# Sums of transformed weights written in place, three accumulating loads under way, and other prices in the order

## The chip, the cores and the metric

The kernel runs on one core of a Trainium2 chip. The metric is the time on the device of one execution, in microseconds (us); the profiled execution's span, from its first instruction to its last, is given beside its time. The engines are TensorE (PE; PEld is its weight loading), VectorE (DVE), ScalarE (ACT), GpSimd (POOL) and SyncE (SP), each with an in-order queue of its own.

## The reference

One step of an encoder of two layers over a prompt of 512 tokens and a sample of 64, which share all weights (width 1024). A layer is an FFN, a mixer with three kinds of attention, attention over a memory of 256 tokens, and a second FFN; outputs are both activations and all new cache entries.

```python
def half_ffn(x, g, w_gate, w_up, w_down):
    h = rms_norm(x, g)
    return 0.5 * ((jax.nn.silu(h @ w_gate) * (h @ w_up)) @ w_down)

x = x + half_ffn(x, p['ffn1_norm'], p['ffn1_w_gate'], p['ffn1_w_up'], p['ffn1_w_down'])
...
x = x + merge_heads(oa, ob, oc, p['b_sub_norm'], p['w_out'], lam_init)
...
x = x + memory_attention(x, mk, mv, p)
x = x + half_ffn(x, p['ffn2_norm'], p['ffn2_w_gate'], p['ffn2_w_up'], p['ffn2_w_down'])
```

Everything is float32. D_FF is 2816, so the four FFNs hold most of the products.

## The kernel before

Activations lie transposed, features on the 128 partitions and the 576 tokens as columns, in two halves of 288. Each float32 factor is split into a high part (float32r, `whi` of a weight, written by a copy) and the rest (`wlo`, a subtraction), and a product is three matmuls: high by high, high by low, low by high. Splitting a weight tile of 512 columns is one copy on ScalarE or VectorE and one subtraction on VectorE; there are eight buffers each for the high and the low parts.

Most FFN products (`gate`, `up` from tile 4 on, and all `down`) multiply 2 x 2 blocks with seven products in place of eight (`wino`): a unit covers a pair of output tiles, and k pairs of input tiles (4 for gate and up, 2 or 3 for down), with n = 128 k columns to a quadrant of its weights. A raw load brings three quadrants (a12, a11, a22) into `stage`, 1536 columns at most, of which there are 2 buffers. A second load brings 2n columns into `wcd` (tag "wc", 2 buffers), and a third, issued by GpSimd, adds the rest of the weights to it under way; that gives c3 and c1. Two sums then make c2 = c1 + a11 and c4 = c2 + a12, into tiles named `wc` that come from the large buffers "b" (11 of 896 columns). The adds may run on VectorE or GpSimd. In the order of the record a unit is: splits of a11 and a12 and their products, the sums, c2, c3, c1, c4, a22. The products go into the banks P, Q and Y; after the first and later products of P its contents are evacuated (`cw`, `dw`, `c` by ScalarE, or a VectorE operation on `x`) before the next product adds to the same bank. In the FFN, eight of the "b" buffers hold the transformed activations `xbh` and `xbl`; in the mixer "b" holds keys and values.

The program is recorded as a list of operations (`Program.op`) and then put in order by a list planner (`Program.order`) that has a price for each operation, a time for each dependence, and the number of buffers of each tag. A step takes the operation that can start first; where an operation may run on two engines, it takes the one that would end first, with 300 ns added for VectorE. Operations of VectorE with two inputs in SBUF, and all that read SBUF on GpSimd, are planned one after another (`port`). A load's data is planned for `late` after its transfer. A `reach` says how far ahead of the oldest open operation a tag's buffers may be taken, by how many are free; names in `free_reach` are exempt, and `quota` bounds how many buffers a name may hold. Weight loads are planned some 9 us ahead of their product, those of `wino` units 3 us more. The order that comes out is issued as it is, and semaphores keep the dependences, so the planner's prices decide the order of each queue and nothing else. All instructions carry line 414, that of `issue`, so the rows are told apart by tiles.

Of the kernel before, what the change touches and what calls it, by code (L numbers as in the profile page):

```python
# [10 lines left out]
F32 = mybir.dt.float32  # L11
F32R = mybir.dt.float32r
AF = mybir.ActivationFunctionType
ALU = mybir.AluOpType
# [4 lines left out]
SP = 512  # L19
# [157 lines left out]
class View:  # L177
# [29 lines left out]
    def split(self, n):  # L207
        (m, st), = self.dims
        return View(self.tile, self.part, self.off, [(n, st * (m // n)), (m // n, st)], self.dtype, self.path + (("split", n),))
# [23 lines left out]
class Program:  # L233


    def __init__(self):
        self.ops = []
        self.pos = 0.0
        self.shift = 0.0
        self.tiles = []  # L240
        self.free_reach = ("wc", "xbh", "xbl")
        self.shared = True
        self.extra = {"DVE": 300.0}
        self.quota = {"wc": 6}
        self.reach = {"s": (-12000.0, 3000.0), "b": (-12000.0, 4000.0)}

    def tile(self, tag, shape, dtype, name):
        t = Tile(tag, shape, dtype, name)
# [36 lines left out]
    def order(self, slots, window=60000.0, depth=24):  # L285
# [8 lines left out]
        def push(o):  # L294
            for e in o.costs:
                heapq.heappush(ready[e], (o.prio, o.start, o))
# [34 lines left out]
        while len(out) < len(self.ops):  # L331
            while byprio[oldest].done:
                oldest += 1
            front = byprio[oldest].prio
            limit = front + window
            best = None
            for e in ENGINES:
                h = ready[e]
                seen, pick = [], None
                while h and len(seen) < depth:  # L340
                    item = heapq.heappop(h)
                    o = item[2]
                    if o.done:
                        continue
                    seen.append(item)
                    if item[0] > limit:
                        break
                    t = estimate(o, e)
                    if t is None:
                        continue  # L350
                    if len(o.costs) > 1:
                        mine = t + o.costs[e] + self.extra.get(e, 0.0)
                        if any(e2 != e and estimate(o, e2) + o.costs[e2] + self.extra.get(e2, 0.0) < mine for e2 in o.costs):
                            continue
                    if pick is None or t < pick[0] - 1.0:
                        pick = (t, o)
                        if t <= free[e] + 1.0:
                            break
                for item in seen:
                    heapq.heappush(h, item)  # L360
                if pick is not None and (best is None or pick[0] < best[0]):
                    best = (*pick, e)
            if best is None:
                names = {}
                for t in self.tiles:
                    if id(t) in place and t.left:
                        names.setdefault(t.tag, {}).setdefault(t.name, 0)
                        names[t.tag][t.name] += 1
                raise RuntimeError(f"no instruction can go on; tiles held: {names}")
            t, o, e = best  # L370
            for x in o.tiles:
                if x.tag is not None and id(x) not in place:
                    heapq.heappop(avail[x.tag])
                    held[x.name] = held.get(x.name, 0) + 1
                if id(x) not in place:
                    place[id(x)] = True
            end = t + o.costs[e]
            free[e] = end
            if e in o.port:
                port = end  # L380
            o.ends = (e, end)
            o.done = True
            out.append((o, e))
            if o.dma:
                dma = max(end + 650.0, dma) + o.extra
                late = 900.0 if e == "SP" else 2900.0
                o.extra = dma + late - end
                end = dma + late
            for x in o.tiles:
                x.last = max(x.last, end)  # L390
                x.left -= 1
                if not x.left and x.tag is not None:
                    heapq.heappush(avail[x.tag], x.last)
                    held[x.name] -= 1
            for u in o.users:
                u.wait -= 1
                if not u.wait:
                    push(u)
# [24 lines left out]


def pool_cost(n):
    return 154 + 2.09 * n


def copy_cost(src):
# [1 line left out]


class Trunk:
    N_S = 46
    N_B = 11
    STAGE = 2
    WC = 2
    WB = 8

    def __init__(self, a):  # L440
# [14 lines left out]
        return self.new("s", [128, T], dt, nm)  # L455

    def bl(self, dt=F32R, nm="b"):
        return self.new("b", [128, 896], dt, nm)

    def tiny(self, nm="t"):  # L460
        return self.new("tiny", [128, 4], F32, nm)
# [113 lines left out]
    def ahead(self):  # L575
        return -self.AHEAD * self.p.pos / (self.p.pos + self.AHEAD) - 900.0
# [43 lines left out]
    def wino(self, movs, sinks):  # L620

        p = self.p
        n = 128 * len(movs)

        def ahead(f, *k, early=0.0):
            keep, p.shift = p.shift, self.ahead() - early
            r = f(*k)  # L630
            p.shift = keep
            return r

        def load():
            raw, _, src = self.fetch()
            c31 = self.new("wc", [128, 1024], F32, "wcd")[:, :2 * n]
            self.load(c31, src[:, n:3 * n])
            src, _, _ = self.unit_source()
            self.gather(c31, src)
            return raw, c31  # L640

        def sums(raw, c31):
            if 2 * n <= 896:
                c24 = self.bl(F32, "wc")
                c2, c4 = c24[:, :n], c24[:, n:2 * n]
            else:
                c2, c4 = self.bl(F32, "wc")[:, :n], self.bl(F32, "wc")[:, :n]
            self.tt(c2, c31[:, n:], raw[:, n:2 * n], ALU.add, self.WADD)
            self.tt(c4, c2, raw[:, :n], ALU.add, self.WADD)
            if 2 * n <= 512:  # L650
                return c24[:, :2 * n],
            return c2, c4

        raw, c31 = ahead(load, early=self.EARLY)
        w = {}

        def split(names, src):
            hi, lo = ahead(self.parts, src)
            for i, nm in enumerate(names):
                w[nm] = hi[:, n * i:n * i + n], lo[:, n * i:n * i + n]  # L660

        def product(ps, nm, i, first, last):
            hi, lo = w[nm]
            for k, mov in enumerate(movs):
                xhi, xlo = mov[i]
                o = slice(128 * k, 128 * k + 128)
                self.mms([(ps, lhs[:, o], x, first and k == 0 and j == 0, last and k == len(movs) - 1 and j == 2, False)
                          for j, (lhs, x) in enumerate(((hi, xhi), (hi, xlo), (lo, xhi)))])

        both = 2 * n <= 512  # L670
        if both:
            split(("a12", "a11"), raw[:, :2 * n])
        else:
            split(("a11",), raw[:, n:2 * n])
        P = self.bank("P")[:, :288]
        product(P, "a11", 0, True, False)
        sinks[0](P)
        if not both:
            split(("a12",), raw[:, :n])
        Q = self.bank("Q")[:, :288]  # L680
        product(Q, "a12", 1, True, True)
        sinks[1](Q)
        c = ahead(sums, raw, c31)
        if both:
            split(("c2", "c4"), c[0])
        else:
            split(("c2",), c[0])
        product(P, "c2", 4, False, False)
        sinks[2](P)
        if both:  # L690
            split(("c3", "c1"), c31)
        else:
            split(("c3",), c31[:, :n])
        Y = self.bank("Y")[:, :288]
        product(Y, "c3", 5, True, False)
        if not both:
            split(("c1",), c31[:, n:])
        product(P, "c1", 3, False, False)
        sinks[3](P, Y)
        if not both:  # L700
            split(("c4",), c[1])
        product(P, "c4", 2, False, True)
        sinks[4](P)
        split(("a22",), raw[:, 2 * n:])
        product(Y, "a22", 6, False, True)
        sinks[5](Y)
# [487 lines left out]
    def mix(self, l):  # L1194
# [50 lines left out]
        self.load(self.rope, a["rope"])  # L1245
        self.maskc = self.sl(nm="maskc")[:, :SP]
        self.load(self.maskc, a["maskc"])
        self.kpe = self.new("wc", [128, 1024], F32, "kpe")
        self.memset(self.kpe[96:128], 0.0, "POOL")
        proj(1)  # L1250
        attend_a(1)
# [15 lines left out]
        for g in range(2, GROUPS):  # L1267
            if g < 4:
# [6 lines left out]
                for ps, c in self.gemm("ukv", u[0], cko, KH):  # L1275
                    n = c.stop - c.start
# [7 lines left out]
                for ps, c in self.gemm("ukv", u[1], cko, KH):  # L1284
                    n = c.stop - c.start
# [151 lines left out]
            self.ffn(l, 2, ("ffn1_norm", l + 1) if l + 1 < DEPTH else None)  # L1437

    def slots(self):
        return {"s": self.N_S, "b": self.N_B, "tiny": 24, "sm": 8, "stage": self.STAGE, "hi": self.WB, "lo": self.WB, "wc": self.WC}  # L1440


def build(tc, a):
# [159 lines left out]
```

## Time and profile before

| what | value |
|---|---|
| time, median of 3 runs | 2491.7 us (2484.65 to 2495.42) |
| profiled execution | 2488.79 us, of it the span 2487.0 us |
| TensorE busy | 2405.7 us, 97% |
| VectorE busy | 2113.8 us, 85% |
| ScalarE busy | 1549.1 us, 62% |
| GpSimd busy | 487.6 us, 20% |
| moved by DMA | 316.00 MB, 127 GB/s |

The busy times are of the profiled execution and overlap; the ends of matmuls are modelled. A stretch is read as its length and, for each engine, the time in which it was busy. The FFN units with sums run in four stretches, about 60 to 416 us, 885 to 1244, 1310 to 1648 and 2116 to 2487; mixer, memory attention and the first FFN tiles lie between.

### The profile page before, as it was taken

To read this page: it belongs to the slowest core of one execution; us is meant where nothing else is said; L and a number is where in the kernel's file an instruction comes from. 1 tells how busy PE (TensorE), PEld (TensorE's weight loads), DVE (VectorE), ACT (ScalarE), POOL (GpSimd) and SP (SyncE) were. 2 spreads that over 40 slices of the span, in tenths; PEclk is the share of its full clock that TensorE was granted. 3 is DMA by queue.
4 is the path that set the end of the run, shared out by engine and by line. 5 is a ranking of instruction groups with operands and counts; after the bars stand their busy time and mean duration, and the time that the engine had idled before them with its cause. 6 is when DMAs were issued, how large, how long until landed. Compare 5 with 4: busy or idle time off the path is not lost.

```text
span 2487.0 us, 46756 instructions
## 1 busy us (share of the span) xinstructions
PE 2405.7 (97%) x17622; PEld 2333.4 (94%) x17622; DVE 2113.8 (85%) x4276; ACT 1549.1 (62%) x3266; POOL 487.6 (20%) x500
## 2 busy tenths in 40 slices
PE   8899999999999999999999999999999999999998
PEld 8899999998999999999999999899989999999998
DVE  8888889789896898888898888896898869888887
ACT  5555666679765755556556555576887566555554
POOL 1122220101120122222112332210112101322220
PEclk9899999999999999999999999999999999999999
DMA  4556565222342245566536566641223322365664
GB/s 154 136 153 157 156 166 155 71 70 78 106 141 77 69 114 145 147 165 177 131 105 162 138 162 159 173 136 64 74 86 116 119 69 79 106 170 142 167 169 118
DMA packets 104242, 316.00 MB, mean 127 GB/s; under 512 B 11856, under 2 KB 16016, under 8 KB 104016
## 3 DMA queue, kind: packets, MB, share of 16 engines
q1 hardware_dynamic: 82128, 252.19, 30.5%
q0 software_dynamic: 21888, 60.83, 14.5%
q8 instruction: 138, 2.26, 0.4%
q14 instruction: 88, 0.72, 0.1%
HBM read 300.11 MB, written 12.86 MB: 126 GB/s over the span
## 4 chain that ended last, share of the span: by engine, by line
PE 58%; DVE 25%; DMA 9%; ACT 5%; issue 2%; POOL 0%; SPq 0%; DVEq 0%; ACTq 0%; POOLq 0%
PE P L414 17%; PE Y L414 8%; DVE wlo L414 7%; PE pj L414 7%; DMA wcd<-wf 5%; PE wo L414 4%; PE Q L414 4%; DMA stage<-wf 3%; DVE c L414 3%; PE mq L414 2%; PE mo L414 2%; PE g L414 2%; DVE x L414 2%; DVE wc L414 2%; PE O L414 2%
## 5 line engine op out<-in xcount | busy, mean ns | idle before, releaser
L414 ACT ACTIVATE whi<-stage 128x512 fp32r<-128x512 f32 (+2 forms) x565 | 335.4, 600 | 297.8 <-PE P L414 76.1
L414 DVE TENSOR_TENSOR wlo<-stage,whi 128x512 fp32r<-128x512 f32 (+2 forms) x658 | 434.4, 672 | 94.3 <-ACT whi L414 90.5
L414 POOL DMA_DIRECT2D wcd<-wf x152 | 134.9, 892 | 676.9 <-DVE wlo L414 292.6
L414 ACT ACTIVATE whi<-wc 128x512 fp32r<-128x512 f32 (+1 forms) x236 | 145.0, 614 | 110.2 <-PE P L414 53.5
L414 ACT ACTIVATE whi<-wcd 128x512 fp32r<-128x512 f32 (+1 forms) x232 | 140.6, 612 | 70.7 <-DMA wcd<-wf 23.9
L414 DVE TENSOR_TENSOR wlo<-wc,whi 128x512 fp32r<-128x512 f32 (+1 forms) x240 | 171.5, 714 | 15.2 <-ACT whi L414 14.4
L414 DVE TENSOR_TENSOR wlo<-wcd,whi 128x512 fp32r<-128x512 f32 (+1 forms) x240 | 169.2, 709 | 11.0 <-ACT whi L414 10.8
L414 PE MATMUL pj<-xhi,whi 128*128 128x288 f32 x576 | 172.0, 299 | 2.7 <-DVE pt L414 2.7
L414 PE MATMUL P<-xbh,whi 128*128 128x288 f32 x576 | 170.6, 296 | 2.9 <-ACT cw L414 1.7
L414 PE MATMUL P<-xbl,whi 128*128 128x288 f32 x576 | 170.0, 295 | 0.3 <-DVE xbl L414 0.3
L414 PE MATMUL P<-xbh,wlo 128*128 128x288 f32 x576 | 170.1, 295 | 0.0
L414 PE MATMUL pj<-xhi,wlo 128*128 128x288 f32 x576 | 169.7, 295 | 0.0
L414 PE MATMUL pj<-xlo,whi 128*128 128x288 f32 x576 | 169.7, 295 | 0.0
L414 POOL TENSOR_TENSOR wc<-wcd,stage 128x256 f32<-128x256 f32 (+2 forms) x71 | 88.0, 1240 | 263.9 <-DMA wcd<-wf 146.0
L414 ACT ACTIVATE dw<-P 128x288 f32<-128x288 f32 x240 | 96.2, 401 | 48.2 <-PE P L414 48.2
L414 PEld LDWEIGHTS P<-xbh,whi 128*128 128x128 f32 x576 | 108.1, 188 | 4.5 <-ACT cw L414 2.7
L414 PEld LDWEIGHTS pj<-xhi,whi 128*128 128x128 f32 x576 | 108.1, 188 | 4.5 <-issue 4.2
L414 ACT ACTIVATE cw<-P 128x288 f32<-128x288 f32 x216 | 85.5, 396 | 41.6 <-PE P L414 41.6
L414 PE MATMUL P<-hbh,wlo 128*128 128x288 f32 x352 | 105.6, 300 | 3.5 <-DVE wlo L414 3.5
L414 PEld LDWEIGHTS P<-xbl,whi 128*128 128x128 f32 x576 | 108.1, 188 | 0.6 <-DVE xbl L414 0.6
L414 PEld LDWEIGHTS pj<-xlo,whi 128*128 128x128 f32 x576 | 108.1, 188 | 0.4
L414 PEld LDWEIGHTS P<-xbh,wlo 128*128 128x128 f32 x576 | 108.2, 188 | 0.0
(495 smaller groups left out, 9435.9 us busy)
## 6 DMA issues: line engine op xcount, KB each, us to landing
stage<-wf SPq DMA_DIRECT2D x125, 512.0 KB, 3.5
stage<-wf SPq DMA_DIRECT2D x72, 768.0 KB, 4.2
wcd<-wf SPq DMA_DIRECT2D x72, 512.0 KB, 3.6
wcd<-wf POOLq DMA_DIRECT2D x72, 512.0 KB, 6.3
stage<-wf SPq DMA_DIRECT2D x68, 384.0 KB, 4.0
wcd<-wf SPq DMA_DIRECT2D x64, 256.0 KB, 2.8
wcd<-wf POOLq DMA_DIRECT2D x64, 256.0 KB, 5.7
stage<-wf SPq DMA_DIRECT2D x16, 576.0 KB, 4.2
```

The source lines that it names most:

```text
L414: getattr(eng[e], fn)(**{n: real(v) for n, v in k.items()})
```

## The change

The buffers of tag "wc" are gone. `wcd` is taken from "b", whose 11 buffers grow from 896 to 1024 columns, at most three of them at a time. The two sums write over the raw quadrants that they read, c2 over a11 and c4 over a12, so their tiles `wc` are gone as well; for small units the split of both takes them in that order. `kpe`, the rotary key of the mixer, moves from "wc" to "b". One more "s" buffer (47) is made. In the planner, loads are taken to land 1000 ns later, GpSimd's elementwise price goes from 154 + 2.09 to 250 + 4.5 ns per column, and the reach of "b" begins at -4000 in place of -12000 ns, so that the last free buffers may be taken earlier.

```diff
--- before.py
+++ after.py
@@ -238,11 +238,11 @@
         self.pos = 0.0
         self.shift = 0.0
         self.tiles = []
-        self.free_reach = ("wc", "xbh", "xbl")
+        self.free_reach = ("wcd", "xbh", "xbl")
         self.shared = True
         self.extra = {"DVE": 300.0}
-        self.quota = {"wc": 6}
-        self.reach = {"s": (-12000.0, 3000.0), "b": (-12000.0, 4000.0)}
+        self.quota = {"wcd": 3}
+        self.reach = {"s": (-12000.0, 3000.0), "b": (-4000.0, 4000.0)}
 
     def tile(self, tag, shape, dtype, name):
         t = Tile(tag, shape, dtype, name)
@@ -383,7 +383,7 @@
             out.append((o, e))
             if o.dma:
                 dma = max(end + 650.0, dma) + o.extra
-                late = 900.0 if e == "SP" else 2900.0
+                late = 1900.0 if e == "SP" else 3900.0
                 o.extra = dma + late - end
                 end = dma + late
             for x in o.tiles:
@@ -423,7 +423,7 @@
 
 
 def pool_cost(n):
-    return 154 + 2.09 * n
+    return 250 + 4.5 * n
 
 
 def copy_cost(src):
@@ -431,10 +431,9 @@
 
 
 class Trunk:
-    N_S = 46
+    N_S = 47
     N_B = 11
     STAGE = 2
-    WC = 2
     WB = 8
 
     def __init__(self, a):
@@ -455,7 +454,7 @@
         return self.new("s", [128, T], dt, nm)
 
     def bl(self, dt=F32R, nm="b"):
-        return self.new("b", [128, 896], dt, nm)
+        return self.new("b", [128, 1024], dt, nm)
 
     def tiny(self, nm="t"):
         return self.new("tiny", [128, 4], F32, nm)
@@ -633,23 +632,17 @@
 
         def load():
             raw, _, src = self.fetch()
-            c31 = self.new("wc", [128, 1024], F32, "wcd")[:, :2 * n]
+            c31 = self.bl(F32, "wcd")[:, :2 * n]
             self.load(c31, src[:, n:3 * n])
             src, _, _ = self.unit_source()
             self.gather(c31, src)
             return raw, c31
 
         def sums(raw, c31):
-            if 2 * n <= 896:
-                c24 = self.bl(F32, "wc")
-                c2, c4 = c24[:, :n], c24[:, n:2 * n]
-            else:
-                c2, c4 = self.bl(F32, "wc")[:, :n], self.bl(F32, "wc")[:, :n]
-            self.tt(c2, c31[:, n:], raw[:, n:2 * n], ALU.add, self.WADD)
-            self.tt(c4, c2, raw[:, :n], ALU.add, self.WADD)
-            if 2 * n <= 512:
-                return c24[:, :2 * n],
-            return c2, c4
+            c4, c2 = raw[:, :n], raw[:, n:2 * n]
+            self.tt(c2, c31[:, n:], c2, ALU.add, self.WADD)
+            self.tt(c4, c2, c4, ALU.add, self.WADD)
+            return c4, c2
 
         raw, c31 = ahead(load, early=self.EARLY)
         w = {}
@@ -680,11 +673,11 @@
         Q = self.bank("Q")[:, :288]
         product(Q, "a12", 1, True, True)
         sinks[1](Q)
-        c = ahead(sums, raw, c31)
+        c4, c2 = ahead(sums, raw, c31)
         if both:
-            split(("c2", "c4"), c[0])
+            split(("c4", "c2"), raw[:, :2 * n])
         else:
-            split(("c2",), c[0])
+            split(("c2",), c2)
         product(P, "c2", 4, False, False)
         sinks[2](P)
         if both:
@@ -698,7 +691,7 @@
         product(P, "c1", 3, False, False)
         sinks[3](P, Y)
         if not both:
-            split(("c4",), c[1])
+            split(("c4",), c4)
         product(P, "c4", 2, False, True)
         sinks[4](P)
         split(("a22",), raw[:, 2 * n:])
@@ -1245,7 +1238,7 @@
         self.load(self.rope, a["rope"])
         self.maskc = self.sl(nm="maskc")[:, :SP]
         self.load(self.maskc, a["maskc"])
-        self.kpe = self.new("wc", [128, 1024], F32, "kpe")
+        self.kpe = self.bl(F32, "kpe")
         self.memset(self.kpe[96:128], 0.0, "POOL")
         proj(1)
         attend_a(1)
@@ -1437,7 +1430,7 @@
             self.ffn(l, 2, ("ffn1_norm", l + 1) if l + 1 < DEPTH else None)
 
     def slots(self):
-        return {"s": self.N_S, "b": self.N_B, "tiny": 24, "sm": 8, "stage": self.STAGE, "hi": self.WB, "lo": self.WB, "wc": self.WC}
+        return {"s": self.N_S, "b": self.N_B, "tiny": 24, "sm": 8, "stage": self.STAGE, "hi": self.WB, "lo": self.WB}
 
 
 def build(tc, a):
```

## Rows read from the trace of the kernel before

**Rows 1.** Page, part 1: busy time of each engine

```profile
PE 2405.7 (97%) x17622; PEld 2333.4 (94%) x17622; DVE 2113.8 (85%) x4276; ACT 1549.1 (62%) x3266; POOL 487.6 (20%) x500
```

**Rows 2.** Stretches; columns: length, busy PE, PEld, DVE, ACT, POOL, clock, DMA share, GB/s

```profile
60.00:416.00 356.00, 337.62 (x2446) 329.23 (x2445) 307.61 (x576) 207.17 (x415) 76.51 (x82) 0.98 0.57 151
885.00:1244.00 359.00, 346.13 (x2531) 338.68 (x2530) 309.00 (x555) 205.24 (x411) 89.56 (x90) 0.99 0.56 148
1310.00:1648.00 338.00, 326.32 (x2380) 318.48 (x2379) 288.80 (x527) 199.32 (x401) 92.19 (x88) 0.99 0.59 153
2116.00:2487.00 371.00, 352.63 (x2578) 344.92 (x2576) 309.28 (x558) 200.22 (x405) 84.65 (x85) 0.99 0.54 145
```

**Rows 3.** Waits of TensorE over the whole span: total us, times, longest

```profile
PE Y L414 <- DVE x L414: 12.1, 19, 1.3
PE P L414 <- ACT dw L414: 11.6, 14, 1.6
PE P L414 <- ACT cw L414: 9.2, 17, 0.8
...
PE P L414 <- DVE wlo L414: 6.2, 10, 1.3
```

**Rows 4.** Chain of waits in 885 to 1244 us, share by line

```profile
by line: PE P L414 26.2%; DMA wcd<-wf 12.6%; PE Y L414 11.7%; DVE wlo L414 9.6%; PE Q L414 5.8%; DMA stage<-wf 4.9%; DVE c L414 4.5%; DVE x L414 3.2%; issue 3.2%; DVE wc L414 3.0%; DVE ht L414 2.6%; ACT whi L414 2.5%; DVE hrl L414 1.6%; DVE
```

**Rows 5.** Pieces of the chain within 1015 to 1075 us: start, length, what

```profile
1022.33 8.85 DMA wcd<-wf
...
1033.72 4.12 DMA stage<-wf
...
1041.58 0.79 PE Q L414 x6
```

**Rows 6.** Timeline of 1026 to 1034 us; in brackets the idle time before it

```profile
1031.21 0.69 DVE L414 TENSOR_TENSOR wc<-wcd,stage 128x512 f32<-128x512 f32 x1 [2.10 <-DMA wcd<-wf]
1031.27 0.63 ACT L414 ACTIVATE whi<-wcd 128x512 fp32r<-128x512 f32 x1 [2.42 <-DMA wcd<-wf]
1031.81 0.39 ACT L414 ACTIVATE dw<-P 128x288 f32<-128x288 f32 x1
...
1031.93 1.17 POOL L414 TENSOR_TENSOR wc<-wcd,stage 128x256 f32<-128x256 f32 x1 [5.38 <-DVE wc L414]
...
1032.25 0.40 PE L414 MATMUL P<-hsh,whi 128*128 128x288 f32 x1 [1.07 <-ACT dw L414]
...
1032.42 1.23 DVE L414 TENSOR_TENSOR wc<-wc,stage 128x512 f32<-128x512 f32 x1
```

**Rows 7.** Waits of SyncE's own queue: total us, times, longest

```profile
SPq L414 <- DVE wlo L414: 1372.4, 294, 17.9
SPq L414 <- DVE wc L414: 527.7, 61, 14.4
```

**Rows 8.** DMA issues: count, KB each, median us to landing

```profile
wcd<-wf SPq DMA_DIRECT2D x72, 512.0 KB, 3.6
wcd<-wf POOLq DMA_DIRECT2D x72, 512.0 KB, 6.3
```

**Rows 9.** Groups by shape, VectorE and GpSimd: count, busy us, mean ns

```profile
L414 DVE TENSOR_TENSOR wlo<-stage,whi 128x512 fp32r<-128x512 f32 x542 | 381.2, 713 | 85.3 <-ACT whi L414 81.9
...
L414 DVE TENSOR_TENSOR wc<-wcd,stage 128x512 f32<-128x512 f32 x59 | 48.9, 828 | 19.5 <-DMA wcd<-wf 19.5
...
L414 DVE TENSOR_TENSOR wc<-wc,stage 128x256 f32<-128x256 f32 x23 | 9.5, 415 | 0.0
...
L414 POOL TENSOR_TENSOR wc<-wcd,stage 128x256 f32<-128x256 f32 x55 | 61.6, 1119 | 198.7 <-DMA wcd<-wf 114.4 <-DVE wc L414 24.1 <-DVE x L414 16.6
```

**Rows 10.** Waits of all engines: total us, times, longest

```profile
POOL wc L414 <- DMA wcd<-wf: 146.0, 38, 7.5
...
ACT whi L414 <- DMA stage<-wf: 60.1, 56, 3.2
...
DVE wc L414 <- DMA wcd<-wf: 26.8, 19, 3.3
```

## The prediction

> **What bounds the kernel now.** I read the profile from the top: busy shares, stretches, TensorE's waits, then the chain of waits where they stand. TensorE is busy for 2405.7 us of 2487.0 us [rows 1], so 81.3 us is the most that any reordering can return; the change removes no product. The stretches say where this idle time lies [rows 2]. The four in which FFN units with sums run, 60 to 416, 885 to 1244, 1310 to 1648 and 2116 to 2487 us, hold 18.4 + 12.9 + 11.7 + 18.4 = 61.3 us; the start, the two mixers and the rest share the other 20.0 us. The granted clock is 0.98 to 1.00 there, the level of 2.4 GHz, so it is no term.
>
> Not all of the 61.3 us can be reached. TensorE's waits [rows 3] show four kinds inside these stretches that repeat: Y for VectorE's `x` (12.1 us), P for ScalarE's `dw` (11.6), P for `cw` (9.2), P for `wlo` (6.2), together 39.1 us. The other 22.2 us are waits of other kinds, such as those of the last chunk, whose products need the h that was just computed; I leave them where they are.
>
> Why are `dw` and `cw` late, if evacuating a bank is a 0.39 us job? The chain of waits in 885 to 1244 us gives the DMA of `wcd` 12.6% and of `stage` 4.9% [rows 4]. One instance shows the mechanism [rows 5, 6]. The accumulating load is issued at 1022.33 and ends 8.85 us later. ScalarE has stood 2.42 us for it, at the head of its in-order queue, with the split of `wcd`. Behind that split stands `dw`, which starts at 1031.81, 0.6 us into a 1.07 us wait of TensorE. VectorE had waited 2.10 us for the same landing and starts its sum 0.03 us after it. So a weight that comes late does not starve TensorE of weights (8 hi/lo slots are ahead of it); it blocks a queue in which an evacuation stands.
>
> The load is late because it starts late. SyncE sits waiting for VectorE's `wlo` 294 times (1372.4 us) and for the sum `wc` 61 times (527.7 us) [rows 7]: `wlo` frees a `wcd` or stage buffer, `wc` a stage buffer. From the plain load's issue to the sum, a 512 KB unit needs 3.6 us for the load and 6.3 us for the accumulating one [rows 8], about 10 us, and with two `wcd` buffers it has only the time of the one unit between. At 0.132 us a matmul (6 of Q in 0.79 us [rows 5]) a unit of two pairs is 7 x 2 x 3 x 0.132 = 5.6 us and one of four pairs 11.1 us. Ten does not fit in 5.6, and barely in 11.1.
>
> **The change, part by part.**
> Third `wcd` buffer: each load may start one unit sooner, 5.6 to 11.1 us, against lateness of 2 to 3 us as in [rows 6]. It reaches the share of the 39.1 us that the wcd DMA leads. On the chain wcd has 12.6% against 4.9% for stage and 9.6% for VectorE's own `wlo` [rows 4]: 12.6 of 27.1, so I take half, 19.5 us. Bounds: nothing, if stage is just as late; 39 us, if stage's lateness (its release waits for the same sum) goes too.
>
> Sums in place: no instruction more or less (152 first and 152 second adds). The adds now must follow the splits of the quadrants they overwrite, which stand before them in the order anyway: nothing. But stage is now held until `c4` has been split, where before the second sum and the split of `a22` freed it. In a four-pair unit c2, c3 and c1 may come first: 3 splits at TensorE's pace of 12 x 0.132 = 1.6 us are 4.8 us, at VectorE's own 0.68 us [rows 6] 2.0 us. SyncE then issues the next raw load that much later; it lands after some 4.1 us [rows 5]. It is covered by the two-pair unit between, 5.6 us, with little to spare. Against this, the sum itself comes up to a unit sooner. I cost it at 2 us lost, 0 to 15.
>
> GpSimd's price (154 + 2.09n to 250 + 4.5n; for 256 columns 689 to 1402 ns, against 65 + 267 + 300 = 632 for VectorE). The old price let GpSimd win whenever VectorE was 57 ns behind, the new one only at 770 ns, longer than the 0.45 us operations that stand in between. I take it that nearly all of the 290 adds and subtracts on GpSimd go to VectorE: 500 instructions [rows 1] less 152 loads, and less 58 casts, copies and memsets that its groups show; the largest group of adds stands in [rows 9]. At VectorE's 0.42 us for 256 columns [rows 9], 0.69 for 512 [rows 6], it is about 0.46 us each by their shapes, most of them 256 and 288: 134 us of VectorE. It gets some back: the sum at 1032.42 beside a GpSimd add took 1.23 us, that at 1031.21 alone 0.69 [rows 6]. Two groups with means of 713 and 828 ns against 0.68 alone give back 542 x 0.031 + 59 x 0.146 = 25 us [rows 9]; with `wlo` of the other sources, the second sums and the smaller groups I take 80, bounds 25 and 134. Net some 54 us more VectorE, most of it in the 1424 us of the four stretches. There it is idle for 1424 - 1215 = 209 us [rows 2], which hides it; if that cover were gone, a fifth (10 us) would come through. I charge 2 us.
>
> A rule of the Trainium skill speaks to this term. "SBUF — State Buffer", section "Who interferes with whom", says that the port pair shared by VectorE and GpSimd is an exclusive lock: the one that comes second blocks for the other's whole instruction. By that, an add that leaves GpSimd could give VectorE back up to its whole 1.1 us instead of 80/290 = 0.3. The instance agrees in kind (0.54 us lost to a GpSimd add that had started first), but the two groups together do not come near 1.1 us for each add.
>
> Loads priced 1.0 us later: for a 512 KB load the planner goes from 650 + 1456 + 900 = 3.0 us to 4.0; seen, 3.6 [rows 8]. The accumulating one, from 6.5 to 7.5; seen, 6.3. Consumers of raw weights get placed later, so that ScalarE's 60.1 us of waiting for stage [rows 10] shrink. Some of that is the same time as above; I add 1.5 us, 0 to 6.
>
> Buffers `b`: 11 as before, but no reserve of two in the planner's rule, and `kpe` takes one, so the mixer has 10 in place of 9. It has its part of the 20.0 us outside the four stretches; I take 1 us, from -3 to +4. In the FFN, 8 are held by `xbh`/`xbl` and 3 remain, just the quota. The 47th `s` buffer: nothing, since no row shows a wait for one.
>
> Sum: -19.5 + 2 + 2 - 1.5 - 1 = -18.0 us. The profiled execution took 2488.8 us (span 2487.0 and 1.8 around it), so 2470.8; its time is 0.12% under the median of 2491.7, which puts the forecast at 2473.7, rounded to 2474.
>
> **Rivals.** One: stage takes over. Its two buffers are untouched, the longer hold eats what the earlier `wcd` gives, and ScalarE stands for `stage` where it stood for `wcd`. For: stage is second on the chain, and in the instance a stage load of 4.12 us follows the wcd load within two microseconds [rows 5]. Against: stage was waiting for the sum, and the sum for `wcd`. Time: no gain, 2491.7 as now. The engines that move the data are busy for 0.54 to 0.59 of these stretches [rows 2], so a third unit under way has room. The Trainium skill ("Trainium Kernel Development and Optimization", section "Key Constraints") has all queues share the same 16 DMA engines, which would make this rival certain only if that share were full.
>
> Two, the other side: VectorE blocks at the sums. GpSimd absorbed 146.0 us of waiting for `wcd` in 38 waits [rows 10], 3.8 us each, with nothing behind it but more GpSimd work. On VectorE everything stands behind such a wait, above all `c` and `x` that empty Y. If the loads are no earlier, each 3.8 us less two products in hand (2 x 1.6) gets through for 0.6 us: 38 x 0.6 = 23 us lost, 2512 on the profile, 2515 on the median. It decides if more than about a third of the gathers still land after VectorE arrives. Against it: the third buffer moves them by 5.6 us or more.
>
> Three: VectorE is truly relieved. If the adds that leave GpSimd give back all that they cost (134 us, the upper bound above) or more, the 39.1 us goes whole, with a fifth of the other 22.2: 39 + 5 = 44 us, 2445 on the profile, 2448 on the median. The lock rule of the Trainium skill ("SBUF — State Buffer", above) leads here.
>
> **How the numbers follow.** Forecast 0.50, its own range 2459 to 2484 (a third to four fifths of the 39.1 us, give or take the small terms); stage takes over 0.25; VectorE blocks 0.13; VectorE relieved 0.12. About 0.5%, 12.5 us, is what a measurement can tell from no change here. Faster than 2479: the third rival and 0.46 of the 0.50, 0.58. Slower than 2504: 0.13, less 0.01 for milder forms, 0.12. The rest, 0.30, is the same. The range runs from the relieved case with a little below it, 2443, to 2500, which holds the stage case and its small losses and leaves out the blocked one.
>
> **What would show it.** Right: three loads of `wcd` under way, sums starting microseconds after landing, not 0.03 us; wcd's share of the chain in the four stretches from over 10% to under 5%; TensorE's waits for `dw`, `cw` and `x` halved; GpSimd near 200 us busy and 210 instructions; VectorE at about 2168 us. Wrong: `stage` leading the chain with more than wcd had, or VectorE's waits for `wcd` well over 26.8 us [rows 10].

## The result and the profile after

The changed kernel takes 2400.63 us (median of 4 runs, 2398.12 to 2400.97), the kernel before on the same chip 2491.45 us (2484.65 to 2495.42): a ratio of 0.9636, 95% interval 0.9614 to 0.9658, or 91 us less. The forecast was 2474 us in a range of 2443 to 2500. The direction was right and the gain five times what was forecast, outside the range.

The page of the changed kernel, part 1 (busy time by engine, counterpart of [rows 1]) and the first line of part 4 (chain that ended last); the last line is that of part 4 in the kernel before:

```profile
PE 2369.9 (99%) x17622; PEld 2323.5 (97%) x17622; DVE 2102.7 (88%) x4496; ACT 1564.0 (65%) x3315; POOL 191.2 (8%) x231
...
PE 90%; DVE 7%; ACT 2%; issue 1%; DMA 0%; SPq 0%; DVEq 0%; ACTq 0%
...
PE 58%; DVE 25%; DMA 9%; ACT 5%; issue 2%; POOL 0%; SPq 0%; DVEq 0%; ACTq 0%; POOLq 0%
```

The span is 2399.2 us. TensorE's idle time went from 81.3 to 29.3 us, 52.0 us less. The span went down by 87.8 us, though: the other 35.8 us came out of TensorE's *busy* time, with the same 17622 matmuls. A small part of that is the clock: the mean granted clock was 0.992 before and 0.997 after, which is about 38 us of the span at the lower level (0.50, 1.2 GHz) before and 15 us after. In the traces 112 matmuls start in those 38 us and 51 in the 15 us; those of 288 columns start 0.24 us apart there, against 0.133 at the full clock, so the clock accounts for some 6 of the 35.8 us. The part on why the prediction was wrong says where the rest was hidden. GpSimd fell to 191.2 us; VectorE did not rise by the 54 us that were forecast, but fell by 11.

The four stretches with sums, now 112 us shorter and cut a little tighter than in [rows 2] (columns as there):

```profile
63.00:395.00 332.00, 327.06 (x2423) 323.83 (x2422) 298.06 (x602) 204.92 (x417) 31.70 (x36) 0.99 0.61 158
...
879.00:1203.00 324.00, 321.90 (x2399) 319.45 (x2398) 289.40 (x568) 200.30 (x405) 30.48 (x35) 0.99 0.62 159
1260.00:1585.00 325.00, 322.43 (x2414) 319.87 (x2413) 292.34 (x578) 204.60 (x415) 31.68 (x36) 1.00 0.62 160
...
2068.00:2399.20 331.20, 325.04 (x2424) 322.74 (x2423) 286.37 (x564) 193.58 (x394) 29.61 (x34) 0.99 0.60 156
```

Since the cuts differ, compare time per matmul: 1424 us for 9935 in [rows 2], 0.1433 us each; 1312.2 us for 9660 here, 0.1358 us each. The difference, 0.0075 us times 9660, is 72 us. So four fifths of the gain lie in these stretches. TensorE is idle there for 15.8 us, where it was for 61.3.

The chain of waits in the second stretch, share by line, with [rows 4] as its counterpart, and one of its longest pieces (start, length, what):

```profile
by line: PE P L414 55.2%; PE Y L414 27.3%; PE Q L414 13.8%; DVE wlo L414 1.1%; DVE c L414 0.5%; issue 0.5%; DVE stage L414 0.4%; DVE ht L414 0.2%; ACT c L414 0.2%; DVE hbl L414 0.2%; DVE hsl L414 0.2%; ACT whi L414 0.2%; DVE x L414 0.1%; AC
...
1152.60 4.78 PE P L414 x36
```

No DMA is left on it: `wcd` had 12.6% and `stage` 4.9%. The chain is now 96% TensorE, 36 matmuls in a row at 0.133 us.

Waits of all engines in the changed kernel (total us, times, longest), with [rows 3, 10] as counterpart:

```profile
ACT whi L414 <- DMA stage<-wf: 8.3, 10, 2.1
...
PE g L414 <- DVE whi L414: 6.9, 1, 6.9
...
DVE whi L414 <- DMA stage<-wf: 5.5, 2, 5.3
...
PE P L414 <- ACT cw L414: 1.0, 2, 0.5
...
PE P L414 <- ACT dw L414: 0.6, 2, 0.3
...
PE Y L414 <- DVE wlo L414: 0.5, 2, 0.3
```

`dw` fell from 11.6 to 0.6 us, `cw` from 9.2 to 1.0, ScalarE's wait for `stage` from 60.1 to 8.3. Neither VectorE nor ScalarE waits for `wcd` at all. What is left for TensorE are single waits, such as one of 6.9 us in front of `g`.

Waits of SyncE's queue, counterpart of [rows 7], show which release now paces the plain loads:

```profile
SPq L414 <- DVE wlo L414: 1656.0, 317, 17.5
SPq L414 <- DVE stage L414: 184.3, 70, 5.1
```

The old wait for the sum `wc`, 527.7 us, is gone; the sum, now called `stage`, holds SyncE for 184.3 us. Loads still wait for room, but in time. The starts in the two traces show it (152 units, matched in order): a unit's plain `wcd` load starts in the median 29.2 us before the unit's first matmul into Q, where it started 17.1 us before it.

### The profile page after: what moved, and what is told of

Same layout as the page of the kernel before. It is cut to its first block, busy times and chain, and to the rows that moved or that the text cites. A ratio compares the mean times of both kernels' runs of the same rounds, so it can differ in the third digit from the quotient of the medians.

```text
span 2399.2 us, 46696 instructions
## 1 busy us (share of the span) xinstructions
PE 2369.9 (99%) x17622; PEld 2323.5 (97%) x17622; DVE 2102.7 (88%) x4496; ACT 1564.0 (65%) x3315; POOL 191.2 (8%) x231
## 4 chain that ended last, share of the span: by engine, by line
PE 90%; DVE 7%; ACT 2%; issue 1%; DMA 0%; SPq 0%; DVEq 0%; ACTq 0%
PE P L414 30%; PE Y L414 15%; PE pj L414 8%; PE Q L414 7%; PE wo L414 4%; PE g L414 4%; PE u L414 3%; PE mq L414 2%; PE mo L414 2%; PE O L414 2%; PE cq L414 2%; PE S L414 1%; DVE wlo L414 1%; PE st L414 1%; PE ckv L414 1%; PE T L414 1%
## 5 line engine op out<-in xcount | busy, mean ns | idle before, releaser
L414 ACT ACTIVATE whi<-stage 128x512 fp32r<-128x512 f32 (+2 forms) x826 | 495.6, 603 | 463.7 <-PE P L414 222.2
L414 DVE TENSOR_TENSOR wlo<-stage,whi 128x512 fp32r<-128x512 f32 (+2 forms) x898 | 581.2, 655 | 132.5 <-ACT whi L414 126.5
L414 ACT ACTIVATE whi<-wcd 128x512 fp32r<-128x512 f32 (+1 forms) x240 | 147.2, 616 | 109.1 <-PE P L414 41.0
L414 DVE TENSOR_TENSOR wlo<-wcd,whi 128x512 fp32r<-128x512 f32 (+1 forms) x240 | 158.4, 668 | 35.6 <-ACT whi L414 35.6
L414 PEld LDWEIGHTS pj<-xhi,wlo 128*128 128x128 f32 x576 | 108.1, 188 | 0.0
L414 PE MATMUL P<-hbl,whi 128*128 128x288 f32 x352 | 104.8, 298 | 1.5 <-DVE hbl L414 1.5
L414 PE MATMUL P<-hbh,whi 128*128 128x288 f32 x352 | 104.3, 296 | 0.6 <-ACT dw L414 0.6
L414 ACT ACTIVATE p<-p,smx 128x512 f32<-128x512 f32 (+3 forms) x174 | 91.4, 554 | 12.9 <-DVE smx L414 12.6
```

The lines of the kernel that those rows point to most:

```text
L414: getattr(eng[e], fn)(**{n: real(v) for n, v in k.items()})
```

## The experiments

Each run is compared with the kernel before on its own chip; ratios have 95% intervals.

**The two halves.** `e1_buffers` is the changed kernel with both old prices, `e2_prices` the kernel before with both new ones.

```diff
 e1_buffers, against the changed kernel
-                late = 1900.0 if e == "SP" else 3900.0
+                late = 900.0 if e == "SP" else 2900.0
-    return 250 + 4.5 * n
+    return 154 + 2.09 * n
 e2_prices, against the kernel before: the reverse
```

> The changed kernel with both old prices back (loads 0.9 and 2.9 us late, GpSimd 154 + 2.09n), so the buffers alone. If the third wcd buffer is the cause (depth), most of the 91 us stays: 2400 to 2420 us. If the prices are (the order), most goes: 2470 to 2490 us. If both are needed, 2430 to 2460 us.

> The kernel before with both new prices and no other edit. Depth: 2475 to 2495 us, since two wcd buffers leave each load as late as it was. Prices: 2400 to 2430 us. Both needed: between, 2440 to 2470 us.

`e1_buffers` took 2428.42 us, ratio 0.976 (0.9734 to 0.9787), 62.6 us less. `e2_prices` took 2421.68 us, 0.9726 (0.9704 to 0.9747), 69.4 us less. Each half alone gives some seven tenths of the 91 us, and neither is the small term that was forecast for the prices. They replace each other in part. The waits of `e2_prices` show one way in which they do:

```profile
ACT whi L414 <- DMA stage<-wf: 42.2, 40, 3.0
...
DVE wc L414 <- DMA wcd<-wf: 1.8, 4, 0.7
...
ACT whi L414 <- DMA wcd<-wf: 0.6, 1, 0.6
```

With two `wcd` buffers as before, VectorE's wait for `wcd` is 1.8 us, where it was 26.8 [rows 10]. The loads start no earlier: the plain `wcd` load starts in the median 13.1 us before its unit's first matmul into Q (17.1 before). But their consumers stand later in the in-order queues: the unit's first sum starts with that matmul, where it started 7.0 us ahead of it. So hardly anything stands behind a landing of `wcd`.

**Which part of the buffers.** `e9_in_place` adds only the sums in place to the kernel before (the hunks of `sums` and the splits), and keeps two buffers of tag "wc".

> The kernel before with the sums in place alone; wcd keeps its two buffers, the prices are old. If the tiles of the sums were short (three b buffers beside xbh and xbl, of which a four-pair unit takes two), this gives most of what the buffers alone gave: 2425 to 2450 us. If the third wcd buffer gave it, 2475 to 2495 us; if the longer hold of stage costs, over 2495 us.

It took 2496.3 us, 1.002 (1.0006 to 1.0034), 6 us more, too little to tell from the scatter of orders shown further down. Its waits are those of the rival in which `stage` takes over, at 108.5 us against 60.1:

```profile
ACT whi L414 <- DMA stage<-wf: 108.5, 84, 4.5
DVE whi L414 <- DMA stage<-wf: 79.0, 69, 5.5
...
PE P L414 <- ACT dw L414: 32.4, 35, 3.0
```

The next runs set the quota of `wcd` to two, with new prices, with old ones, and with old ones and 46 `s` buffers.

```diff
 e3_two_units, e10_buffers_two (old prices too), e17_two_s46 (old prices and N_S = 46 too)
-        self.quota = {"wcd": 3}
+        self.quota = {"wcd": 2}
```

> The changed kernel with the quota of wcd at 2 in place of 3; sums in place and prices stay. Depth: 2465 to 2495 us, and wcd back on the chain of waits with more than 5%. Prices: 2400 to 2415 us. If two buffers with the stage held longer are worse than before, over 2495 us.

> The changed kernel with both old prices and two wcd buffers. At old prices the third buffer is what the buffers' 63 us come from: 2475 to 2500 us, like the sums in place alone. If it is the room in b (reach, kpe, the 47th s), 2425 to 2445 us, like the buffers alone.

> The changed kernel with both old prices, two wcd buffers and 46 s buffers; what is left beside the sums in place is the reach of b and the place of kpe. If the 47th s buffer is the cause of the 53 us, 2475 to 2500 us. If not, 2435 to 2450 us.

They took 2410.34 us, 0.9685 (0.9665 to 0.9706); 2442.76 us, 0.9801 (0.9778 to 0.9825); and 2420.01 us, 0.9719 (0.9699 to 0.9739): 81, 50 and 70 us less. Read alone, that says that the third buffer is worth 10 to 12 us or nothing. But the quota counts the planner's units and does not take the buffer away. So two more runs made ten `b` buffers out of eleven; `xbh` and `xbl` hold eight in the FFN, and two are left.

```diff
 e19_b10 (new prices), e20_buffers_b10 (old prices), against the changed kernel
-    N_B = 11
+    N_B = 10
```

> The changed kernel with 10 b buffers, so that two are left for wcd in the FFN (and one less in the mixers). If the third buffer is what the buffers bring, it costs more than the 10 us of the quota even at the new prices: 2415 to 2440 us, the loss in the FFN stretches. If it is not, 2400 to 2412 us.

> The same at the old prices, beside the buffers alone (2428) and the sums in place alone (2496). If the third buffer gave the 63 us, 2475 to 2500 us. If something else in the buffers did, 2425 to 2445 us.

`e19_b10` took 2470.62 us, 0.9918 (0.9892 to 0.9943), 19.5 us less; `e20_buffers_b10` 2499.15 us, 1.0046 (1.0028 to 1.0063), 9 us more. Beside the same kernels with eleven (90.8 and 62.6 us less) both lose some 71 us. SyncE's timeline tells the two ways to have "two" apart (start, length, what). First `e3_two_units`:

```profile
986.60 0.33 SPq L414 DMA_DIRECT2D stage<-wf  x1
987.02 0.38 SPq L414 DMA_DIRECT2D wcd<-wf  x1
...
1000.31 0.33 SPq L414 DMA_DIRECT2D stage<-wf  x1
1000.73 0.38 SPq L414 DMA_DIRECT2D wcd<-wf  x1
```

And `e19_b10`:

```profile
982.98 0.33 SPq L414 DMA_DIRECT2D wcd<-wf  x1
983.94 0.33 SPq L414 DMA_DIRECT2D stage<-wf  x1
...
999.51 0.33 SPq L414 DMA_DIRECT2D wcd<-wf  x1
1000.06 0.33 SPq L414 DMA_DIRECT2D stage<-wf  x1
```

In the first, `wcd` follows its `stage` load by 0.4 us: a buffer has long been free, and only the stage buffer was waited for. In the second the order is turned round; the next raw load stands behind a `wcd` load that had to wait for its own buffer. SyncE's waits say the same over the whole span. In `e19_b10` it waits for landings of `wcd`, and in `e3_two_units` it never does:

```profile
SPq L414 <- DMA wcd<-wf: 337.5, 57, 11.0
```

So the quota of two left the loads early, 25.0 us before the unit's first matmul into Q in the median, and ten buffers made them late, 19.0 us. The waits of `e19_b10` show who pays, close to the numbers of before:

```profile
ACT whi L414 <- DMA stage<-wf: 69.2, 57, 5.0
DVE whi L414 <- DMA stage<-wf: 20.5, 23, 5.0
PE P L414 <- ACT dw L414: 13.7, 15, 3.4
...
PE P L414 <- ACT cw L414: 11.6, 15, 3.5
```

And so does its first stretch, 0.147 us a matmul, where the changed kernel has 0.137 (columns as in [rows 2]):

```profile
63.00:420.00 357.00, 338.23 (x2426) 329.89 (x2425) 307.88 (x629) 191.71 (x391) 30.60 (x35) 0.98 0.56 145
```

All four stretches take 1373.6 us there for 9672 matmuls, 0.1420 us each against 0.1358: some 60 of the 70 us that it is slower than the changed kernel lie in them. That matters, because the eleventh buffer is missing in the mixers too. A third buffer with the sums not in place was not tried.

**Which price.** One price at a time, put back in the changed kernel (`e4_old_pool`, `e5_old_late`) or put into the kernel before (`e6_pool_only`, `e7_late_only`), by the same lines as above.

> The changed kernel with GpSimd's old price alone; some 290 adds go back to GpSimd. Depth: 2400 to 2415 us, as VectorE's net load hardly differs. If the adds on GpSimd were what made banks late, 2440 us or more.

> The changed kernel with the loads' old lateness (0.9 and 2.9 us) and the rest as changed. Placement (a load's consumers queued before it lands are what holds up the evacuations): 2425 to 2445 us, near the buffers alone. GpSimd's price was the useful one of the two: 2400 to 2415 us.

> The kernel before with GpSimd's new price alone. Placement by the loads' price: 2470 to 2490 us, with VectorE now waiting for wcd itself. GpSimd's price: 2420 to 2440 us, and VectorE's waits for wcd under 10 us.

> The kernel before with the loads' new lateness alone. Placement: 2420 to 2445 us, with ScalarE's 60.1 and 23.9 us of waits for stage and wcd down to under a half. GpSimd's price: 2470 to 2490 us.

| run | us | ratio (95%) | against before |
|---|---|---|---|
| `e4_old_pool` | 2410.77 | 0.9686 (0.9665 to 0.9707) | -80.3 us |
| `e5_old_late` | 2417.73 | 0.9708 (0.9693 to 0.9722) | -72.4 us |
| `e6_pool_only` | 2440.82 | 0.9805 (0.9789 to 0.9821) | -49.3 us |
| `e7_late_only` | 2461.02 | 0.9884 (0.987 to 0.9899) | -29.1 us |

GpSimd's price is worth 49 us on the old buffers and 10 on the new ones, the load's 29 and 18. In `e6_pool_only` VectorE waits for `wcd` longer than before, 38.2 us against 26.8, and the kernel is still 49 us faster:

```profile
DVE wc L414 <- DMA wcd<-wf: 38.2, 24, 3.4
```

So what helps there is not the landing. `e11_same_order` takes the planner out: the kernel before, with its order as planned, but each of GpSimd's 290 elementwise instructions issued on VectorE at the place in the order that it had.

```diff
-                getattr(eng[e], fn)(
+                getattr(eng["DVE" if e == "POOL" and fn == "tensor_tensor" else e], fn)(
```

> The kernel before in its own planned order, with old prices and buffers; only at issue are the elementwise operations of two inputs that were planned on GpSimd put on VectorE, in their places. If GpSimd's adds cost by their own slowness and by holding up VectorE, 2435 to 2455 us, as with its new price alone (2441). If the new price worked by giving another order, 2480 to 2495 us. If VectorE is too full for them, over 2495 us.

It took 2459.77 us, 0.9867 (0.9841 to 0.9894), 33.1 us less. Part 1 of its page:

```profile
PE 2394.3 (97%) x17622; PEld 2332.6 (95%) x17622; DVE 2113.3 (86%) x4566; ACT 1549.6 (63%) x3266; POOL 161.4 (7%) x210
```

VectorE has 290 instructions more than in [rows 1] and is busy for 2113.3 us against 2113.8: no time more at all. Two of its groups by shape (count, busy us, mean ns, idle before) say where the time came back, against [rows 9]:

```profile
L414 DVE TENSOR_TENSOR wlo<-stage,whi 128x512 fp32r<-128x512 f32 x542 | 368.7, 690 | 84.5 <-ACT whi L414 80.8 <-PE P L414 0.4
...
L414 DVE TENSOR_TENSOR wc<-wcd,stage 128x512 f32<-128x512 f32 x72 | 49.5, 688 | 31.5 <-DMA wcd<-wf 31.3
```

The same subtract went from 713 to 690 ns, the same sum from 828 to 688.

**How far the prices carry.** `e12_later` prices loads another 1.0 us later than the change does; `e13_vector_price` raises VectorE's fixed price instead.

```diff
 e12_later, against the changed kernel
-                late = 1900.0 if e == "SP" else 3900.0
+                late = 2900.0 if e == "SP" else 4900.0
 e13_vector_price, against the changed kernel: VectorE's fixed part, at both places
-65
+150
```

> The changed kernel with loads priced a further 1.0 us later (2.9 and 4.9). Placement, if lateness is still short of what is seen: 2392 to 2399 us. If it is enough, 2398 to 2405 us. If a later price wastes buffers, over 2405 us.

> The changed kernel with VectorE's elementwise price raised from 65 to 150 ns and the column rate kept, so that 512 columns cost 685 ns as they do on the chip. If honest prices are what the change brought, 2385 to 2398 us. If what is left does not lie in the order, 2398 to 2405 us.

`e12_later` took 2403.04 us, 0.9643 (0.9622 to 0.9664), the same as the changed kernel: a still later price has nothing more to give. `e13_vector_price` took 2470.02 us, 0.9914 (0.9889 to 0.9939), 69 us more than the changed kernel, with the same buffers. Its waits:

```profile
PE P L414 <- ACT xbh L414: 13.3, 4, 3.4
ACT whi L414 <- DMA stage<-wf: 12.8, 15, 2.5
PE P L414 <- ACT cw L414: 8.2, 15, 0.9
PE Q L414 <- ACT xsh L414: 6.9, 4, 2.2
```

The loads are in time (12.8 us against 60.1). TensorE waits for ScalarE, which is busy for 1590.9 us, 27 more than in the changed kernel. And its mean granted clock is 0.985, against 0.997: some 73 us of the span at the lower level in place of 15, which is worth 29 us at most. Why this order makes TensorE wait, and so the cause of these 69 us, is open.

**Small terms and how much an order scatters.** `e15_s46` has 46 `s` buffers, `e16_reach` only the new reach of `b` on the kernel before, `e18_nudge` only loads priced 0.1 us later there.

```diff
 e15_s46, against the changed kernel
-    N_S = 47
+    N_S = 46
 e16_reach, against the kernel before
-        self.reach = {"s": (-12000.0, 3000.0), "b": (-12000.0, 4000.0)}
+        self.reach = {"s": (-12000.0, 3000.0), "b": (-4000.0, 4000.0)}
 e18_nudge, against the kernel before
-                late = 900.0 if e == "SP" else 2900.0
+                late = 1000.0 if e == "SP" else 3000.0
```

> The changed kernel with 46 s buffers in place of 47. If the s buffer carries the FFN's gain, 2420 to 2450 us. If the prices make up for it, 2400 to 2412 us.

> The kernel before with the reach of b from -4000 alone. Only the mixers use it: 2480 to 2492 us, gained in the two mixer stretches. If it is the reach that gave the 53 us, 2430 to 2450 us.

> The kernel before with loads priced 0.1 us later in place of 1.0. If the time follows the price, 2485 to 2490 us, a tenth of the 29 us. If any new order moves the time by tens of us, it lies more than 10 us from the kernel before, on either side.

`e15_s46` took 2406.34 us, 0.9669 (0.9654 to 0.9684), 6 us more than the changed kernel; `e16_reach` 2491.7 us, 1.0013 (1.0 to 1.0025), nothing; `e18_nudge` 2480.74 us, 0.9964 (0.9948 to 0.998), 9 us less. A nudge that means nothing moves the order by 9 us, and `e17_two_s46`, with one buffer fewer than `e10_buffers_two`, was 20 us faster. So I read no difference under some 20 us between two orders as a mechanism: the 47th `s` buffer, the quota and what each price is worth by itself on the new buffers (10 and 18 us) stay unsettled. The 69 us of `e13_vector_price` show that a new order can also cost more than that. The 71 us of the third buffer therefore rest on having come out twice, at two sets of prices, and on the waits that came with them, and not on their size alone.

## Why the prediction was wrong in size

In short: the ceiling, "81.3 us is the most that any reordering can return", was false, since the span fell by 87.8 us. The term of the third buffer, -19.5 us, was cut out of that ceiling and measured -71. The terms of the two prices, +2 and -1.5 us, measured -28 together beside the new buffers and -69 without them.

**What held.** A `wcd` load that lands late blocks ScalarE and VectorE's queues, and TensorE waits for the evacuation behind it. The signs named for it came: no `wcd` on the chain, `dw` and `cw` down by nine tenths, GpSimd at 191.2 us and 231 instructions (forecast: near 200 and 210), and the first sum 19.4 us behind the issue of the accumulating load in the median (6.7 before), whose landing takes 5.7 us for 512 KB. The 71 us that come back when the third buffer is taken away, twice, show that this mechanism was most of the matter.

**The ceiling failed.** "81.3 us is the most that any reordering can return" reads idle time as all the time that a wait costs. TensorE's timeline in the kernel before, at the wait of [rows 6]:

```profile
1030.75 0.29 PE L414 MATMUL P<-xbl,whi 128*128 128x288 f32 x1
1030.88 0.30 PE L414 MATMUL P<-xbh,wlo 128*128 128x288 f32 x1
1032.25 0.40 PE L414 MATMUL P<-hsh,whi 128*128 128x288 f32 x1 [1.07 <-ACT dw L414]
1032.49 0.30 PE L414 MATMUL P<-hsl,whi 128*128 128x288 f32 x1
```

A matmul is shown for 0.29 us, though the next starts 0.13 us after it. When one must wait, the last 0.16 us of its forerunner count as busy; and the one after the wait is 0.24 us ahead of its successor, not 0.13. The wait shown as 1.07 us cost 1.37 - 0.13 = 1.24, and 0.11 more at the start. Many waits too short to show as idle cost as well. By pace the ceiling comes out otherwise: at 0.1328 us a matmul (36 in 4.78 us) the four stretches of [rows 2] lost 1424 - 9935 x 0.1328 = 105 us, where idle time shows 61.3; the changed kernel lost 1312.2 - 9660 x 0.1328 = 29 us. It takes all matmuls there as of one shape and is an estimate, but it holds the 72 us found above, which the 39.1 us "reachable" could not. Over the whole of both traces, with each matmul's distance to the next taken against the median for its width, 126 us are lost before and 37 after. The difference, 88 us, is what the span fell by. By an estimate from the same starts, about 12 us of the 35.8 were hidden under forerunners' records, 7 were slower restarts, 7 waits too short to show, and 9 lay in the stretches at the lower clock, 6 of them by the clock itself. The prediction had put the clock down as "no term"; its part was small.

**The third buffer's term failed in size:** half of 39.1 us, at most 39, was forecast, 71 measured. Beside the ceiling, the split by shares of the chain was wrong. It took half of the lateness for `stage`'s own; but SyncE issues both loads in one queue, and a `wcd` load that waits for a buffer holds the next raw load behind it (`e19_b10`). One cause stood under two names, which the upper bound did consider.

**Sums in place:** +2 us, 0 to 15; measured +6 (`e9_in_place`) and +9 (`e20_buffers_b10`), in the range. The first rival's mechanism, `stage` held longer and waited for instead, shows in the waits of `e9_in_place`; the time by itself lies within the scatter. The third buffer lifts it, in the changed kernel to 8.3 us.

**GpSimd's price:** +2 us was charged, since 290 adds would cost VectorE 134 us and give back 80. They give back all they cost, the upper bound, and VectorE's net was -11 us instead of +54. The premise of the third rival was right. Of the 49 us on the old buffers, 33 appear with the order untouched (`e11_same_order`); the other 16 lie within the scatter of orders. Whether the 33 us come from the hindrance to VectorE or from GpSimd's own slow adds (1119 ns for one of 256 columns [rows 9], 419 to 422 on VectorE) was not taken apart. On the new buffers some 10 us are left, which the scatter could hide.

The lock rule of the Trainium skill ("SBUF — State Buffer", section "Who interferes with whom") has the second of the two engines block for the other's whole instruction, where VectorE's has two inputs in SBUF and GpSimd's reads SBUF. The trace agrees in kind. In size, 134 us (an estimate) for 290 adds is 0.46 us each, some two fifths of the 1.1 us that an add held GpSimd.

**The second rival fell.** VectorE did wait longer for `wcd` in `e6_pool_only`, by 11 us, with a gain all the same, and in the changed kernel it does not wait for it.

**Loads priced later:** -1.5 us, 0 to -6; measured -29 alone and -18 in the changed kernel. The step counted only ScalarE's wait for `stage`. A later price also puts the sums and splits of `wcd` later in the queues (VectorE waits for `wcd` 1.0 us in `e7_late_only`, 26.8 before [rows 10]), which removes the same blocked queue as the buffer does.

**The sum by measured terms:** sums in place +9, third buffer -71, both prices on the new buffers -28 (`e1_buffers` to the changed kernel): -90 us, against the 91 measured. These are the steps of one path, from the kernel before by `e20_buffers_b10` and `e1_buffers` to the changed kernel, so that they add up is no proof; the first step holds the new reach, `kpe` and the 47th `s` buffer as well. Taken alone, the halves would add up to 132 us; they share 41. By the single prices, GpSimd's loses 39 us of its worth beside the new buffers (49 to 10) and the loads' 11 (29 to 18). Only for the loads' price do the waits show how it does the buffer's work; why GpSimd's price is worth so little beside the buffers was not taken apart.

## What to carry to other kernels

Take the ceiling of a reordering from pace (time per instruction in a stretch against the best run of the same instructions), not from idle time, when the records of a pipelined engine overlap. Where a late load blocks an in-order queue, a deeper buffer and other prices in the planner can cure part of the same loss (63 and 69 us alone, 91 together here), so cost the first one in full and the second only for what is left; and before a run counts as "without the buffer", look in the queue that issues the loads for whether it waits for one. Change the plan by a trifle once, to learn how far orders scatter, before small differences are read.

## What the runs showed of the hardware

An elementwise add on GpSimd relieved VectorE of nothing: 290 of them moved over, at some 0.46 us each, and VectorE's busy time stayed at 2113 us, because its own operations got shorter, such as those of 512 columns from 713 and 828 to 690 and 688 ns. And TensorE's busy time contains waiting: it fell by 35.8 us with the same 17622 matmuls. Some 6 us of that are the clock (mean granted 0.992 before, 0.997 after); the rest is about 0.16 us for each wait that is gone, the slower restart behind it (0.24 us to the next start in place of 0.13), and waits too short to show.
